# A two-layer transformer on one core: attention's outputs leave in three parts, the sums end later, the last heads go by block

## The chip, the core and the metric

One NeuronCore of a Trainium2 runs the whole program in one launch. Its engines each execute their own instructions in order and wait for each other by semaphores: TensorE (PE, matrix products), VectorE (DVE), ScalarE (ACT), GpSimd (POOL), and SyncE (SP), which here only issues transfers. Transfers (DMA) between memory (HBM) and on-chip SBUF run beside them. TensorE writes its products to PSUM, eight banks of 512 float32 a partition; GpSimd does not read PSUM in this program. The metric is the device time of one execution, the median of the runs.

## What is computed

Float32 throughout. An even layer over 2048 tokens (width 1024) with a context of 256 tokens that serves as extra keys, then an odd layer. In the even layer there are 8 heads with keys of their own (A) and 8 heads that share two sets of keys (B):

```python
sc = jnp.einsum('bqhgd,bthd->bhgqt', qi, k).astype(jnp.float32) * scale
p = jax.nn.softmax(sc, axis=-1).astype(v.dtype)
return jnp.einsum('bhgqt,bthe->bqhge', p, v)
...
merged = jnp.concatenate([o_a * jax.nn.silu(g_a), o_b * jax.nn.silu(g_b)], axis=-1)
return merged @ w_out
...
x_new = layer_norm(DEEPNORM_ALPHA * x + gate * y, ln_g, ln_b)
```

The odd layer is `chunk_gmlp`: `u`, `v`, `g` from one projection, a layer norm on `v`, a 128x128 mix of tokens inside each chunk, `u * mixed * silu(g)`, an output projection, again residual and layer norm.

## The kernel before

**Three stages.** `phase1` makes all projections of the even layer (keys, values, queries, gates) and leaves them in HBM. `attention` runs 64 groups, each a head `h` and a block of 512 queries `g`: first 32 groups of the 8 A heads ("first kind"), then 32 of the 8 B heads ("second kind"). `phase3` runs over 4 blocks of 512 tokens: even output projection, odd layer, output.

**Precision.** A float32 product is made of several passes of a rounded type: an operand is split into a high part and the rest (`split`: ACT rounds and DVE subtracts, or POOL does both), and the products high x high, high x low and low x high are added in PSUM.

**A group in `attention`.** The 2304 keys are 18 tiles of 128. For a tile `t`, `score` does three products (A) or two (B) of 512 columns into a PSUM tile `s` (three buffers); ACT takes the exponential twice, into `ph` (rounded) and back into `s` (exact); `low` has DVE subtract them into `pl`. That frees the score's tile. `mul`, four tiles later, multiplies values with both: `oh<-ph` (128 rows: the high part of the values in one half, the rest in the other) and `ol<-pl` (65 rows: a column of ones stands behind the values, so that row 64 collects the sum of the probabilities). The high parts' sum comes either from one more product with a matrix of ones (`ol<-ph,last`) or from GpSimd, which adds the `ph` tiles up (`add`, `sa<-sa,ph`) and splits the result at the end (`total`: sh by ACT, sl by POOL); PE then multiplies sh and sl with the ones at the end of `mul`'s last tile. Which tiles go which way stands in `shares`: its first list are tiles whose split GpSimd makes instead of DVE (`pf`, two operations), its second those that GpSimd adds; the last four groups have neither.

**The maxima.** A softmax needs its row's maximum ahead of the exponential. While group i-1 runs, PE makes plain products of group i's queries with its keys, 18 tiles `m` in two PSUM buffers (`peak`), and DVE takes maxima (`top`). After the last, DVE makes `nm`, which SP writes to HBM (`NM<-nm`, 512 separate elements) and reads back as a row of the query tile (`row`, `q<-NM`); the score products take it in as one more row (the only product of an A tile that needs it is the first, of a B tile the second).

**The end of a group.** `take` copies `ol` to `ob` (ACT), `finish` adds both halves of `oh` to it (two DVE operations), multiplies with the gate (POOL; the gate was loaded by SP) and SP writes the sums to `SU` and the output to `O`. When the last head is through a block of queries, `recip` loads that block's sums of all heads, inverts them (DVE) and writes `R1`. For block 0, `z_load` fetches output and inverse sums and `z_split` (POOL) multiplies and splits them, still inside `attention`.

**Order.** All of this is written as units with a time in tiles: `at(time, f, ...)`; the units are sorted by time and emitted. `InOrder` ties an engine's instructions into exactly that order, for PE, DVE, ACT and POOL. SP's transfers and all of `phase3` are ordered by the framework's own scheduler (by readiness and priority).

**`phase3`.** `weights` loads 512 KB of weights into `w` (two buffers) and splits it into `wh` (ACT) and `wl` (DVE), three buffers each; a tile serves 24 products. In `odd_in`, 16 such steps `j` follow; during them, the next block's outputs are fetched on GpSimd's queue (`z_load`), multiplied with the inverse sums and split (`z_split`, here on DVE), eight slices a block.

## Time and profile before

| | |
|---|---|
| three runs | 3239.22, 3242.19, 3242.39 us, median 3242.19 |
| the profiled execution | 3241.65 us, its span 3239.8 us, clock 0.994 |
| busy | PE 98%, DVE 77%, ACT 60%, POOL 46% of the span |

In forty slices of 81 us (a digit is the busy share in tenths) the stages can be told apart: `phase1` up to slice 8, attention to slice 28, with GpSimd busy, then `phase3`:

```profile
PE   7999999999999999999999999999999999999998
PEld 3887777777777777776666666666788888888886
DVE  4947794688898889888999999998655854855746
ACT  3544453377777777777777777777444353353352
POOL 2000100089999999998888888874100100100000
PEclk9999999999999999999999999999999999999999
DMA  6456746623212232122111111112633533533322
```

Line 636 in the profile stands for all of attention's ordered instructions (they go through one helper); tiles tell them apart. "PEld" is the loading of a matmul's fixed operand, which runs ahead of the product; a wait often stands there.

### The profile page before, as it was taken

What the parts mean: (1) busy time and instruction counts of PE and PEld (TensorE: products, weight loads), DVE (VectorE), ACT (ScalarE), POOL (GpSimd) and SP (SyncE); (2) the same over time, 40 slices, a digit from 0 to 9 for tenths busy, and PEclk for the clock granted to TensorE, in tenths of its full rate; (3) what the DMA queues carried; (4) which work ended last, traced back from release to release, by engine and by line L of the source; (5) the groups of instructions that cost most, each with busy time, mean ns of one, the idle gap of its engine ahead of it and who ended that gap; (6) DMA issues with size and microseconds to landing.
All of it is one profiled execution on the core that took longest, in us unless ns stands there. A gap on an engine that the chain in (4) does not pass through costs nothing.

```text
span 3239.8 us, 40308 instructions
## 1 busy us (share of the span) xinstructions
PE 3162.1 (98%) x13698; PEld 2422.8 (75%) x13698; DVE 2492.7 (77%) x3747; ACT 1935.2 (60%) x3306; POOL 1477.3 (46%) x1249
## 2 busy tenths in 40 slices
PE   7999999999999999999999999999999999999998
PEld 3887777777777777776666666666788888888886
DVE  4947794688898889888999999998655854855746
ACT  3544453377777777777777777777444353353352
POOL 2000100089999999998888888874100100100000
PEclk9999999999999999999999999999999999999999
DMA  6456746623212232122111111112633533533322
GB/s 239 141 170 192 249 158 212 177 69 66 62 38 49 62 65 46 41 62 62 30 29 25 30 47 30 30 25 61 172 98 111 151 110 111 163 101 114 117 91 72
DMA packets 187056, 314.08 MB, mean 97 GB/s; under 512 B 53264, under 2 KB 79184, under 8 KB 184928
## 3 DMA queue, kind: packets, MB, share of 16 engines
q1 hardware_dynamic: 178558, 283.62, 30.8%
q0 software_dynamic: 8000, 27.81, 2.9%
q8 instruction: 108, 1.77, 0.3%
q14 instruction: 100, 0.82, 0.1%
q10 hardware_dynamic: 290, 0.07, 0.0%
HBM read 240.71 MB, written 70.73 MB: 96 GB/s over the span
## 4 chain that ended last, share of the span: by engine, by line
PE 59%; DMA 13%; issue 12%; POOL 8%; DVE 7%; ACT 2%; SPq 0%; POOLq 0%; ACTq 0%; DVEq 0%
PE s L636 12%; DMA NM<-nm 7%; POOL sa L636 6%; PE ol L636 5%; PE ps L193 4%; PE ps L194 4%; PE ps L195 4%; PE oh L636 4%; PE m L636 4%; PE acc L967 3%; PE acc L968 3%; PE acc L969 3%; PE acc L1064 3%; PE acc L1062 3%; PE acc L1063 3%
## 5 line engine op out<-in xcount | busy, mean ns | idle before, releaser
L636 POOL TENSOR_TENSOR sa<-sa,ph 128x512 f32<-128x512 f32 x728 | 939.1, 1290 | 60.3 <-ACT ph L636 14.5
L636 PE MATMUL s<-q,k 96*128 96x512 f32 (+2 forms) x2880 | 873.9, 399 | 31.0 <-DVE pl L636 18.9
L636 ACT ACTIVATE ph<-s 128x512 fp32r<-128x512 f32 x1064 | 633.9, 596 | 303.7 <-PE s L636 284.4
L636 DVE TENSOR_TENSOR pl<-s,ph 128x512 fp32r<-128x512 f32 x1064 | 728.1, 685 | 109.0 <-ACT s L636 85.9
L636 DVE TENSOR_REDUCE mx<-m 128x1 f32<-128x512 f32 x1124 | 763.5, 681 | 57.8 <-PE m L636 54.1
L636 PEld LDWEIGHTS s<-q,k 96*128 96x128 f32 (+2 forms) x2880 | 537.3, 189 | 244.1 <-DVE pl L636 41.9
L636 ACT ACTIVATE s<-s 128x512 f32<-128x512 f32 x1064 | 632.8, 595 | 0.0
L636 PE MATMUL oh<-ph,v 128*128 128x512 f32 x1152 | 454.9, 395 | 0.0
L636 PE MATMUL ol<-pl,v 128*65 128x512 f32 x1152 | 454.8, 395 | 0.0
L636 PE MATMUL m<-k,q 128*128 128x512 f32 (+1 forms) x1250 | 449.1, 376 | 0.0
L67 ACT ACTIVATE wh<-w 128x1024 fp32r<-128x1024 f32 x153 | 162.1, 1060 | 455.0 <-PE acc L969 216.9
L68 DVE TENSOR_TENSOR wl<-w,wh 128x1024 fp32r<-128x1024 f32 x153 | 186.9, 1221 | 244.7 <-ACT wh L67 244.1
L636 PEld LDWEIGHTS m<-k,q 128*128 128x128 f32 (+1 forms) x1250 | 234.3, 189 | 67.5 <-DVE mx L636 14.5
L636 PEld LDWEIGHTS oh<-ph,v 128*128 128x128 f32 x1152 | 218.1, 189 | 48.9
L194 PE MATMUL ps<-xl,wh 128*128 128x512 f32 x608 | 238.4, 392 | 3.4 <-DVE xl L185 3.4
L193 PE MATMUL ps<-xh,wh 128*128 128x512 f32 x608 | 238.5, 393 | 2.9 <-POOL xh L184 2.9
L195 PE MATMUL ps<-xh,wl 128*128 128x512 f32 x608 | 237.8, 391 | 0.0
L636 PEld LDWEIGHTS ol<-pl,v 128*65 128x65 f32 x1152 | 157.5, 137 | 49.7 <-ACT ob L636 0.3
L967 PE MATMUL acc<-wh,k 128*128 128x512 f32 x384 | 152.6, 398 | 0.5 <-ACT v L1031 0.5
L968 PE MATMUL acc<-wl,k 128*128 128x512 f32 x384 | 152.4, 397 | 0.0
L969 PE MATMUL acc<-wh,k 128*128 128x512 f32 x384 | 151.6, 395 | 0.0
L194 PEld LDWEIGHTS ps<-xl,wh 128*128 128x128 f32 x608 | 114.6, 188 | 29.9 <-DVE xl L185 6.0
(319 smaller groups left out, 5054.6 us busy)
## 6 DMA issues: line engine op xcount, KB each, us to landing
w<-in_wug SPq DMA_DIRECT2D x64, 512.0 KB
wr<-in_w SPq DMA_DIRECT2D x38, 512.0 KB
w<-in_e_w_out SPq DMA_DIRECT2D x32, 512.0 KB
w<-in_o_w_in SPq DMA_DIRECT2D x32, 512.0 KB
w<-in_o_w_out SPq DMA_DIRECT2D x32, 512.0 KB
wr<-in_e_w_mod SPq DMA_DIRECT2D x24, 512.0 KB
wr<-in_o_w_mod SPq DMA_DIRECT2D x24, 512.0 KB
q<-QB SPq DMA_DIRECT2D x96, 128.0 KB
```

The source lines that it names most:

```text
L67: e.nc.scalar.activation(h, src, AF.Copy)
L68: e.nc.vector.tensor_tensor(out=l, in0=src, in1=h.bitcast(F32), op=ALU.subtract)
L193: nc.tensor.matmul(out, lhsT=wh(k), rhs=xh(k), start=i == 0, stop=False)
L194: nc.tensor.matmul(out, lhsT=wh(k), rhs=xl(k), start=False, stop=False)
L195: nc.tensor.matmul(out, lhsT=wl(k), rhs=xh(k), start=False, stop=i == n - 1)
L636: i = getattr(self.engine, name)(*args, **kw)
L967: nc.tensor.matmul(ps[t], lhsT=h[:, ts], rhs=w[0][:, k, :], start=first, stop=False)
L968: nc.tensor.matmul(ps[t], lhsT=h[:, ts], rhs=w[1][:, k, :], start=False, stop=False)
L969: nc.tensor.matmul(ps[t], lhsT=l[:, ts], rhs=w[0][:, k, :], start=False, stop=last)
L1062: nc.tensor.matmul(ps, lhsT=w[0][:, k, :], rhs=h, start=k == 0, stop=False)
L1063: nc.tensor.matmul(ps, lhsT=w[0][:, k, :], rhs=l, start=False, stop=False)
L1064: nc.tensor.matmul(ps, lhsT=w[1][:, k, :], rhs=h, start=False, stop=k == NK - 1)
```

## The change

1. *Sums.* `shares` has one list: GpSimd adds tiles 0 to 16 of a first-kind group and 0 to 15 of a second-kind one, and splits no tile (`pf` is gone; every tile has two exponentials and DVE's `pl`). `total` comes three tiles later. Its two products with the ones no longer go into `ol`: 9.1 tiles behind the last addition `sums` makes them in a PSUM tile of the maxima's ring (`m`, two buffers), ACT copies the row out (`os`) and SP writes it to a second array, `SU[1]`.
2. *Outputs.* `take` copies `ol` and SP writes it, with the sums of `ol`, to `O[0]` and `SU[0]`. One tile later `take_high` copies `oh` (ACT) and its halves go to `O[1]` and `O[2]`. DVE's two additions, GpSimd's product and the gate load are gone. `z_more` loads `O[1]`, `O[2]` and the gate of a slice (3 x 256 KB), and `z_split` has four operations ahead of the split where it had one: add, add, gate, inverse sum. In `phase3` the loaded tile `zx` has one buffer and its loads go on GpSimd's queue.
3. *Order.* The last four heads run block by block, their keys loaded once. Their `recip` is in two: the loads, and five tiles later addition, inversion and write (0.1 tiles later for the last block). Block 0's `z_load` and `z_split` start about a group earlier. SP's transfers in attention are held in the order of the units too.
4. *Last stage.* `wl` has two buffers instead of three; the residual's scale and shift move from the steps `j` to the evacuation of `v`; the steps at which slices are split are spread out (`zj`).

Beside this a constant of ones is set directly, and `ph` and `pl` have 9 buffers instead of 11.

```diff
-    q = queue or e.nc.sync
+    q = queue or e.sp
     t = t.bitcast(F32)
-    q.dma_start(t[:, :, 1, :], e.O[i * P:(i + n) * P, cs].rearrange("(k p) t -> p k t", p=P))
+    q.dma_start(t[:, :, 1, :], e.O[0][i * P:(i + n) * P, cs].rearrange("(k p) t -> p k t", p=P))
     for u in range(2):
         r = e.R1[2 * i:2 * (i + n), cs].rearrange("(k u) t -> u k t", u=2)[u]
         q.dma_start(t[u * DV:(u + 1) * DV, :, 0, :], r.partition_broadcast(DV))
 
 
-def z_split(e, hl, z, pool=False):
-    nc = e.nc
+def z_more(e, b, k, sp, queue=None, bufs=1):
+
+    t = sp.tile([P, 3, CH], F32, name="zx", tag="zx", bufs=bufs)
+    for i, src in enumerate(e.O[1:] + [e.G]):
+        (queue or e.sp).dma_start(t[:, i, :], src[k * P:(k + 1) * P, b * CH:(b + 1) * CH])
+    return t
+
+
+def z_split(e, hl, more, z, pool=False):
+
     h, l = hl
-    (pool or nc.vector).tensor_tensor(out=z, in0=l.bitcast(F32), in1=h.bitcast(F32), op=ALU.mult)
+    on = pool or e.nc.vector
+    on.tensor_tensor(out=z, in0=l.bitcast(F32), in1=more[:, 0, :], op=ALU.add)
+    on.tensor_tensor(out=z, in0=z, in1=more[:, 1, :], op=ALU.add)
+    on.tensor_tensor(out=z, in0=z, in1=more[:, 2, :], op=ALU.mult)
+    on.tensor_tensor(out=z, in0=z, in1=h.bitcast(F32), op=ALU.mult)
     split(e, h, l, z, pool)
...
-    PE, DVE, ACT, POOL = (InOrder(tc, x) for x in (nc.tensor, nc.vector, nc.scalar, nc.gpsimd))
-    LAG, LAGP = 4, 8
+    PE, DVE, ACT, POOL, SP = (InOrder(tc, x) for x in (nc.tensor, nc.vector, nc.scalar, nc.gpsimd, nc.sync))
+    e.sp = SP
+    LAG = 4
...
-        work = [(h, g) for h in range(2 * NH) for g in range(NG)]
+
+        work = [(h, g) for h in range(2 * NH - 4) for g in range(NG)]
+        work += [(h, g) for g in range(NG) for h in range(2 * NH - 4, 2 * NH)]
...
             if i >= NW - NG:
-                return (), ()
-            if i < NH * NG:
-                return (4,), tuple(t for t in range(17) if t != 4)
-            return (2, 8), tuple(t for t in range(16) if t not in (2, 5, 8, 12))
+                return ()
+            return tuple(range(17)) if i < NH * NG else tuple(range(16))
 
         def fetch_keys(h):
-            kv[h] = keys(e, h) if h < NH or h % 4 == 0 else kv[h - 1]
+            kv[h] = keys(e, h)
+            if h >= NH:
+                kv.update({k: kv[h] for k in range(h, h + 4)})
...
-            ph = sp.tile([P, CH], F32R, name="ph", tag="ph", bufs=LAGP + 3)
-            pl = sp.tile([P, CH], F32R, name="pl", tag="pl", bufs=LAGP + 3)
-            if t in shares(i)[0]:
-                ps, pf = sp.tile([P, CH], F32, name="pf", tag="pf", bufs=2), ps
-                ACT.activation(ps, pf, AF.Exp)
-            else:
-                ACT.activation(ph, ps, AF.Exp)
-                ACT.activation(ps, ps, AF.Exp)
+            ph = sp.tile([P, CH], F32R, name="ph", tag="ph", bufs=LAG + 5)
+            pl = sp.tile([P, CH], F32R, name="pl", tag="pl", bufs=LAG + 5)
+            ACT.activation(ph, ps, AF.Exp)
+            ACT.activation(ps, ps, AF.Exp)
             pts[s] = (ph, pl, ps)
 
         def low(s):
-            i, t = divmod(s, NTT)
             ph, pl, p = pts[s]
-            if t in shares(i)[0]:
-                POOL.tensor_scalar(out=ph, in0=p, scalar1=1.0, scalar2=0.0, op0=ALU.mult, op1=ALU.add)
-                POOL.tensor_tensor(out=pl, in0=p, in1=ph.bitcast(F32), op=ALU.subtract)
-            else:
-                DVE.tensor_tensor(out=pl, in0=p, in1=ph.bitcast(F32), op=ALU.subtract)
+            DVE.tensor_tensor(out=pl, in0=p, in1=ph.bitcast(F32), op=ALU.subtract)
 
         def add(s):
             i, t = divmod(s, NTT)
-            adds = shares(i)[1]
+            adds = shares(i)
...
-            if t not in shares(i)[1]:
+            if t not in shares(i):
                 PE.matmul(ol[:DV + 1], lhsT=last[:, :DV + 1], rhs=ph, start=False, stop=False)
             if end:
-                for p in tot.pop(i, ()):
-                    PE.matmul(ol[:DV + 1], lhsT=last[:, :DV + 1], rhs=p, start=False, stop=False)
                 PE.matmul(ol[:DV + 1], lhsT=V[:, t, DV:2 * DV + 1], rhs=pl, start=False, stop=True)
 
+        def cell(i):
+            h, g = work[i]
+            return h, slice(g * CH, (g + 1) * CH)
+
         def take(i):
-            ob = outs[i] = sp.tile([P, CH], F32, name="ob", tag="ob", bufs=2)
-            ACT.activation(ob[:DV + 1], acc[i][1][:DV + 1], AF.Copy)
-
-        def finish(i):
-            h, g = work[i]
-            cs = slice(g * CH, (g + 1) * CH)
-            ob, (oh, ol) = outs.pop(i), acc.pop(i)
-            DVE.tensor_tensor(out=ob[:DV], in0=oh[:DV], in1=ob[:DV], op=ALU.add)
-            DVE.tensor_tensor(out=ob[:DV], in0=oh[DV:], in1=ob[:DV], op=ALU.add)
-            POOL.tensor_tensor(out=ob[:DV], in0=ob[:DV], in1=gates.pop(i)[:DV], op=ALU.mult)
-            q = nc.scalar if i == NW - 1 else nc.sync
-            q.dma_start(e.SU[h:h + 1, cs], ob[DV:DV + 1])
-            (nc.gpsimd if i >= NW - NG else q).dma_start(e.O[h * DV:(h + 1) * DV, cs], ob[:DV])
+
+            (h, cs), (oh, ol) = cell(i), acc.pop(i)
+            rows = slice(h * DV, (h + 1) * DV)
+            q = nc.scalar if i == NW - 1 else SP
+            ob = sp.tile([P, CH], F32, name="ob", tag="ob", bufs=2)
+            ACT.activation(ob[:DV + 1], ol[:DV + 1], AF.Copy)
+            q.dma_start(e.SU[0][h:h + 1, cs], ob[DV:DV + 1])
+            q.dma_start(e.O[0][rows, cs], ob[:DV])
+            outs[i] = oh
+
+        def take_high(i):
+            (h, cs), oh = cell(i), outs.pop(i)
+            rows = slice(h * DV, (h + 1) * DV)
+            oc = sp.tile([P, CH], F32, name="oc", tag="oc", bufs=2)
+            ACT.activation(oc, oh, AF.Copy)
+            q = nc.gpsimd if i >= NW - NG else SP
+            for u in range(2):
+                q.dma_start(e.O[1 + u][rows, cs], oc[u * DV:(u + 1) * DV])
+
+        def sums(i):
+
+            pm = pp.tile([P, CH], F32, name="m", tag="m", bufs=2)
+            for u, p in enumerate(tot.pop(i)):
+                PE.matmul(pm[:DV + 1], lhsT=last[:, :DV + 1], rhs=p, start=u == 0, stop=u == 1)
+            tot[i] = pm
+
+        def sums_out(i):
+            h, cs = cell(i)
+            os = sp.tile([P, CH], F32, name="os", tag="os", bufs=2)
+            ACT.activation(os[DV:DV + 1], tot.pop(i)[DV:DV + 1], AF.Copy)
+            SP.dma_start(e.SU[1][h:h + 1, cs], os[DV:DV + 1])
 
         def recip(b):
 
             view = lambda t: t[:, b * CH:(b + 1) * CH].rearrange("h (p j) -> h p j", p=8)
-            rs = sp.tile([P, CH // 8], F32, name="rs", tag="rs", bufs=2)
-            q = nc.scalar if b == NG - 1 else nc.sync
-            q.dma_start(rs, view(e.SU))
-            nc.vector.reciprocal(rs, rs)
+            rs, r2 = rsums[b] = [sp.tile([P, CH // 8], F32, name="rs", tag="rs", bufs=4) for i in range(2)]
+            q = nc.scalar if b == NG - 1 else SP
+            q.dma_start(rs, view(e.SU[0]))
+            n = P if b < NG - 1 else P - 32
+            q.dma_start(r2[:n], view(e.SU[1])[:n // 8])
+
+        def recip_end(b):
+            view = lambda t: t[:, b * CH:(b + 1) * CH].rearrange("h (p j) -> h p j", p=8)
+            rs, r2 = rsums.pop(b)
+            q = nc.scalar if b == NG - 1 else SP
+            n = P if b < NG - 1 else P - 32
+            DVE.tensor_tensor(out=rs[:n], in0=rs[:n], in1=r2[:n], op=ALU.add)
+            DVE.reciprocal(rs, rs)
             q.dma_start(view(e.R1), rs)
...
+            adds = shares(i)
             at(s, score, s)
-            at(s + (0.9 if t in parts else 1.6), low, s)
+            at(s + 1.6, low, s)
             if t in adds:
                 at(s + 1.0, add, s)
             if adds and t == adds[-1]:
-                at(s + 1.1, total, i)
-            place = s + (LAGP if t in parts else LAG + (LATE[t] if t < len(LATE) else 0))
+                at(s + 4.1, total, i)
+                at(s + 9.1, sums, i)
+                at(s + 9.6, sums_out, i)
+            place = s + LAG + (LATE[t] if t < len(LATE) else 0)
             at(place + 0.7, mul, s)
             if t == NTT - 1:
                 at(place + 0.9, take, i)
-                at(place + 2.3, finish, i)
+                at(place + 1.9, take_high, i)
         for b in range(NG):
-            at((NW - NG + b + 1) * NTT + LAG + 2.6, recip, b)
+            time = (NW - 4 * (NG - 1 - b)) * NTT + LAG + (2.6 if b == NG - 1 else 6.1)
+            at(time, recip, b)
+            at(time + (0.1 if b == NG - 1 else 5), recip_end, b)
 
         end = NW * NTT
 
@@ -872,20 +908,28 @@
             e.Z.append(ring(e, more))
 
         e.Z = []
-        at(end - (NG - 1) * NTT - 1, place, False)
+        at(end - NG * NTT - 3, place, False)
         for k in range(3):
-            at(end - (NG - 1) * NTT + 9 + 4 * k, lambda k: z_load(e, 0, e.Z[0].groups[k]), k)
+            at(end - NG * NTT - 2 + 2 * k, lambda k: z_load(e, 0, e.Z[0].groups[k]), k)
 
         at(end - (NG - 2) * NTT + 0.8, lambda: extend(e.Z[0], spare(e)))
         at(end - (NG - 2) * NTT + 1, lambda: z_load(e, 0, e.Z[0].groups[3]))
+        more = {}
+
+        def other(k):
+            more[k] = z_more(e, 0, k, sp, bufs=2)
+
         for k in range(NK):
-            at(end - (NG - 1) * NTT + 4 * k + 17, lambda k: z_split(e, e.Z[0][k], sp.tile([P, CH], F32, name="zt", tag="zt", bufs=2), POOL), k)
+            time = end - NG * NTT + 7 * k + 8
+            at(time - 3, other, k)
+            at(time, lambda k: z_split(e, e.Z[0][k], more.pop(k), sp.tile([P, CH], F32, name="zt", tag="zt", bufs=1), POOL), k)
 
         e.marks = []
         for k in range(3):
             at(end - NTT + 5 * k, lambda: e.marks.append(POOL.last))
         for _, _, (f, *args) in sorted(units):
             f(*args)
+        e.sp = nc.sync
...
-            return wp.tile([P, 1024], F32R if q else F32, name="w" + q, tag="w" + q, bufs=3 if q else 2)
+            return wp.tile([P, 1024], F32R if q else F32, name="w" + q, tag="w" + q, bufs=3 if q == "h" else 2)
...
+                if cc == 0:
+                    nc.vector.tensor_tensor(out=T[:, t, :], in0=T[:, t, :], in1=C["eg"], op=ALU.mult)
+                    nc.vector.tensor_tensor(out=T[:, t, :], in0=T[:, t, :], in1=C["eb"], op=ALU.add)
...
+            zj = (2, 3, 5, 6, 8, 10, 12, 14)
...
-                    if 2 <= j < 10:
-                        z_split(e, Z[j - 2], tmp("y", 3))
+                    if j in zj:
+                        k = zj.index(j)
+                        z_split(e, Z[k], more, tmp("y", 3))
+                        if k + 1 < NK:
+                            more = z_more(e, b + 1, k + 1, wp, nc.gpsimd)
                     if j < len(Z.groups):
                         z_load(e, b + 1, Z.groups[j], nc.gpsimd)
-                if 4 <= j < 12:
-                    t = (j - 4) // 2
-                    nc.vector.tensor_tensor(out=T[:, t, :], in0=T[:, t, :], in1=C["eb" if j % 2 else "eg"], op=ALU.add if j % 2 else ALU.mult)
...
-    e.O = tc.dram_tile([D, SEQ], F32, name="O")
-    e.SU = tc.dram_tile([2 * NH, SEQ], F32, name="SU")
+    e.O = [tc.dram_tile([D, SEQ], F32, name="O%d" % i) for i in range(3)]
+    e.SU = [tc.dram_tile([2 * NH, SEQ], F32, name="SU%d" % i) for i in range(2)]
```

## Rows read from the trace of the kernel before

**Rows 1.** Busy time by stretch: us, busy us (x instructions) of PE, PEld, DVE, ACT, POOL; clock; DMA
```profile
1029.51:1081.68 52.17, 52.17 (x229) 40.23 (x228) 46.90 (x76) 39.87 (x74) 48.66 (x40) 1.00 0.22 47
1578.76:1675.87 97.11, 94.60 (x401) 67.41 (x401) 90.23 (x149) 76.72 (x144) 81.58 (x69) 1.00 0.12 28
2260.00:2280.00 20.00, 17.39 (x68) 11.96 (x68) 9.51 (x15) 13.06 (x25) 9.69 (x8) 0.91 0.22 63
2580.00:2600.00 20.00, 20.00 (x87) 15.98 (x87) 19.61 (x28) 9.14 (x14) 3.49 (x7) 1.00 0.75 235
2281.00:3239.80 958.80, 941.45 (x4192) 765.10 (x4191) 593.31 (x805) 394.57 (x532) 40.57 (x68) 0.99 0.40 119
```
**Rows 2.** Waits, 1554 to 2163 us: total us, times, longest us
```profile
PEld s L636 <- DVE pl L636: 24.4, 25, 1.0
...
PEld s L636 <- DMA q<-NM: 10.4, 16, 0.9
```
**Rows 3.** Timeline of PE: start, us, operation, [idle before and its releaser]
```profile
1810.59 0.50 PE L636 MATMUL s<-q,k 65*128 65x512 f32 x1 [0.23 <-DMA q<-NM]
...
1814.20 0.63 PE L636 MATMUL s<-q,k 128*128 128x512 f32 x2
...
1819.73 0.50 PE L636 MATMUL s<-q,k 128*128 128x512 f32 x1 [0.51 <-DVE pl L636]
```
**Rows 4.** Timeline of DVE, same group
```profile
1817.56 1.40 DVE L636 TENSOR_TENSOR ob<-oh,ob 64x512 f32<-64x512 f32 x2
1818.98 0.69 DVE L636 TENSOR_TENSOR pl<-s,ph 128x512 fp32r<-128x512 f32 x1
...
1822.70 0.17 DVE L636 TENSOR_REDUCE nm<-mx 128x4 fp32r<-128x20 f32 x1
```
**Rows 5.** The chain that ended last, 1797 to 1812 us: start, us, what
```profile
1798.29 0.19 DVE nm L636
...
1798.49 8.54 DMA NM<-nm
...
1807.04 3.51 DMA q<-NM
```
**Rows 6.** GpSimd's additions in the page's groups: busy us, mean ns
```profile
L636 POOL TENSOR_TENSOR sa<-sa,ph 128x512 f32<-128x512 f32 x728 | 939.1, 1290 | 60.3 <-ACT ph L636 14.5
```
**Rows 7.** Timeline of ACT, the group of rows 3
```profile
1816.74 0.59 ACT L636 ACTIVATE ph<-s 128x512 fp32r<-128x512 f32 x1
1817.22 0.59 ACT L636 ACTIVATE s<-s 128x512 f32<-128x512 f32 x1
```
**Rows 8.** Timeline of SyncE's queue in a first-kind head, issue times
```profile
977.36 0.42 SPq L672 DMA_DIRECT2D NM<-nm  x1
977.89 0.56 SPq L574 DMA_DIRECT2D v<-VA  x1
986.62 0.22 SPq L574 DMA_DIRECT2D q<-NM  x1
```
**Rows 9.** Timeline of DVE in the last group
```profile
2267.12 0.55 DVE L832 RECIPROCAL rs<-rs 128x64 f32<-128x64 f32 x1 [4.02 <-DMA rs<-SU]
```
**Rows 10.** Timeline of PE in the last group
```profile
2252.48 0.51 PE L636 MATMUL s<-q,k 65*128 65x512 f32 x1 [1.54 <-DMA q<-NM]
...
2268.27 0.93 PE L636 MATMUL s<-q,k 128*128 128x512 f32 x2 [2.19 <-DVE pl L636]
```
**Rows 11.** Timeline of SyncE's queue, a weight load at a block boundary
```profile
2566.15 0.37 SPq L941 DMA_DIRECT2D w<-in_o_w_in  x1
```
**Rows 12.** Timeline of DVE in a quiet stretch of the last stage
```profile
2413.84 1.23 DVE L68 TENSOR_TENSOR wl<-w,wh 128x1024 fp32r<-128x1024 f32 x1 [4.21 <-ACT wh L67]
```
**Rows 13.** Timeline of ACT, the conversion that uses the load of rows 11
```profile
2579.94 1.06 ACT L67 ACTIVATE wh<-w 128x1024 fp32r<-128x1024 f32 x1 [1.98 <-DMA w<-in_o_w_in]
```
**Rows 14.** DMA issues: KB each, median us from issue to landing
```profile
v<-in_x POOLq DMA_DIRECT2D x8, 512.0 KB, 6.2
...
k<-O POOLq DMA_DIRECT2D x3, 1024.0 KB, 11.0
```

More of the change, by code (lines that the diff above doesn't have):

```diff
@@ L48, in consts @@
     nc.sync.dma_start(e.ident, I["ident"])
-    e.ones = g.tile([P, P], F32, name="ones")
-    nc.vector.memset(e.ones, 1.0)
     e.epsq = {S: g.tile([P, 1], F32, name="eps%d" % i) for i, S in enumerate((1.0, SA, SB))}
@@ L100, in phase1 @@
         ones = cp.tile([P, P], F32R, name="ones")
-        nc.scalar.activation(ones, e.ones, AF.Copy)
+        nc.vector.memset(ones.bitcast(F32), 1.0)
         pick = cp.tile([P, 2, 2], F32, name="pick")
@@ L563, in z_load @@
         q.dma_start(t[u * DV:(u + 1) * DV, :, 0, :], r.partition_broadcast(DV))
-def z_split(e, hl, z, pool=False):
-    nc = e.nc
-    h, l = hl
-    (pool or nc.vector).tensor_tensor(out=z, in0=l.bitcast(F32), in1=h.bitcast(F32), op=ALU.mult)
+def z_more(e, b, k, sp, queue=None, bufs=1):
[4 more added lines that the diff above has]
+def z_split(e, hl, more, z, pool=False):
+    h, l = hl
+    on = pool or e.nc.vector
[3 more added lines that the diff above has]
+    on.tensor_tensor(out=z, in0=z, in1=h.bitcast(F32), op=ALU.mult)
     split(e, h, l, z, pool)
 def load(e, dst, src):
-    e.nc.sync.dma_start(dst.bitcast(F32), src)
+    e.sp.dma_start(dst.bitcast(F32), src)
 def keys(e, h, parts=3, KV=None):
@@ L671, in peak_maxima @@
         DVE.tensor_reduce(out=nm, in_=stats.pop(i), axis=AX.X, op=ALU.max, negate=True)
-        e.nc.sync.dma_start(e.NM[i:i + 1, :].rearrange("o (j p) -> p (o j)", p=P), nm.bitcast(F32))
+        e.sp.dma_start(e.NM[i:i + 1, :].rearrange("o (j p) -> p (o j)", p=P), nm.bitcast(F32))
 def peak_row(e, h, i, Q):
@@ L705, in attention @@
         NG = SEQ // CH
-        work = [(h, g) for h in range(2 * NH) for g in range(NG)]
+        work = [(h, g) for h in range(2 * NH - 4) for g in range(NG)]
+        work += [(h, g) for g in range(NG) for h in range(2 * NH - 4, 2 * NH)]
         NW = len(work)
-        kv, qs, stats, pms, pts = {}, {}, {}, {}, {}
+        kv, qs, stats, pms, pts, rsums = {}, {}, {}, {}, {}, {}
         acc, tot, gates, outs = {}, {}, {}, {}
@@ L794, in mul @@
             if t == 0:
-                gates[i] = sp.tile([P, CH], F32, name="gt", tag="gt", bufs=2)
-                nc.sync.dma_start(gates[i][:DV], e.G[h * DV:(h + 1) * DV, g * CH:(g + 1) * CH])
                 acc[i] = [pp.tile([P, CH], F32, name="o" + q, tag="o" + q, bufs=1 + (q == "h")) for q in "hl"]
@@ L844, in attention @@
                 at((i - 2) * NTT + 1.2, fetch_queries, i)
-            if i % NG == 1 and i // NG + 1 < 2 * NH:
-                at(i * NTT + 1.2, fetch_keys, i // NG + 1)
+            h = i // NG + 1
+            if i % NG == 1 and (h <= NH or h == NH + 4):
+                at(i * NTT + 1.2, fetch_keys, h)
             for m in range((NTT, AHEAD)[i] if i < 2 else 0, NTT):
@@ L853, in attention @@
             i, t = divmod(s, NTT)
-            parts, adds = shares(i)
+            adds = shares(i)
             at(s, score, s)
-            at(s + (0.9 if t in parts else 1.6), low, s)
+            at(s + 1.6, low, s)
             if t in adds:
@@ L1077, in odd_in @@
                 if b + 1 < NB:
-                    if 2 <= j < 10:
-                        z_split(e, Z[j - 2], tmp("y", 3))
+                    if j in zj:
[3 more added lines that the diff above has]
+                            more = z_more(e, b + 1, k + 1, wp, nc.gpsimd)
                     if j < len(Z.groups):
                         z_load(e, b + 1, Z.groups[j], nc.gpsimd)
-                if 4 <= j < 12:
-                    t = (j - 4) // 2
-                    nc.vector.tensor_tensor(out=T[:, t, :], in0=T[:, t, :], in1=C["eb" if j % 2 else "eg"], op=ALU.add if j % 2 else ALU.mult)
+                    if j == 0:
+                        more = z_more(e, b + 1, 0, wp, nc.gpsimd)
             gated(7, st)
@@ L1152, in program @@
     e.nc, e.ins, e.out = nc, ins, out
+    e.sp = nc.sync
     with tile.TileContext(nc) as tc:
```

## The prediction

> **What bounds the kernel now.** The page comes first, but its busy shares settle little: a matmul's record runs past the issue of the next, so a busy PE can hide a wait. I therefore counted issues by stretch. Two groups of a first-kind head take 52.17 us for 228 matmuls (the row's count has one of the next group), 8 of them half wide, so 224 full ones at 0.233 us; PE is busy throughout, it alone sets the time. Four groups of a second-kind head take 97.11 us for 400 matmuls, 392 full ones, which at 0.233 us need 91.3 us: each group takes 24.28 us and loses 1.45 us. The last stage, 959 us, has PE busy 941 us: PE is the bound there [rows 1].
>
> Next the waits of PE in 25 second-kind groups: score products wait for VectorE's (DVE's) `pl`, since a score's PSUM tile is free only after it, and for the row of maxima, `q<-NM` [rows 2]. The timeline of one group places them: 0.51 us idle before the product at 1819.73, and a second product at 1810.59 behind the row [rows 3]. The first is DVE's: it does the two `ob` additions (1.40 us) and only then `pl` at 1818.98 [rows 4]. The second is a chain of transfers: `nm` at 1798.29, its transfer 8.54 us, reading it back 3.51 us; the product goes 12.30 us behind `nm` [rows 3, 5]. The next `nm` comes 12.11 us after that product [rows 3, 4], and 12.11 + 12.30 is the group's 24.41 us. So a second-kind group is a ring: product, `nm`, two transfers, next product. A saving counts in full between the product and `nm`; between `nm` and the next product it only lengthens the wait.
>
> **First-kind heads.** GpSimd (POOL) adds 17 tiles' probabilities instead of 16, so one ones-product goes: 112 full matmuls become 111, 0.233 us in each of 32 groups, **-7.5 us**. PE stays the bound if the others fit into 25.9 us. GpSimd will have 16 additions and the tail's difference, an operation of the same form, 17 x 1.29 = 21.9 us [rows 6]. ScalarE (ACT) issues every 0.48 to 0.49 us [rows 7]; 40 operations (36 exponentials, sh, ob, oc, os) are 19.6 us. Without that cover each us over 25.9 counts 32 times. The saved product lies behind `nm`, but the ring has slack here: the row's transfer took 9.26 us even with the loading of a head's keys and values around it [rows 8], and at PE's own pace there are 25.9 us to go round.
>
> **Second-kind heads.** Four ones-products go (tiles 2, 5, 8 and 12 are now added too): 94 full matmuls, 21.9 us. GpSimd fits with 16 x 1.29 = 20.6 us. DVE swaps two `ob` additions for two `pl`, 37 operations either way. But the four products lie between `nm` and the next product, where the ring has no use for them: nothing by themselves. What counts is `nm`, and I follow it from the score of tile 3 (1814.20; call it 0, then `nm` was at 8.50 [rows 3, 4]). The tail's two products are later now, so score 4 goes at 1.40 instead of 1.84. ScalarE does ob, the two exponentials of tile 4, oc, and those of tiles 5 and 6 at 0.49 us apart; tile 4's second ends at 3.28. DVE, without `ob`, does pl 4 at 3.3, the maximum at 3.9, pl 5 at 4.9 (ScalarE is late by its oc), a maximum, pl 6 at 6.1, the last maximum at 6.85 and `nm` at 7.55. On the way the sums take one of the two maxima tiles: the next product needs the other, which DVE has read at 4.65 and PE wants at 4.19, 0.45 us of PE wait that DVE's own chain mostly covers. So `nm` comes 0.95 us earlier. Bounds: at best the whole 1.40 us of the `ob` additions; at worst the two extra copies before that point (0.98) and the 0.45 us take it all, and it comes 0.03 us later. I take 0.93, the chain's value with a little off. The transfers I leave at 12.3 us: SyncE had an O part and the gate load ahead of NM, it will have three O parts and a second row of sums. 27 steady groups: **-25.1 us** (from +1 to -38). A group is then 23.35 us where PE needs 21.9 + 0.5, so its wait at the row grows to some 0.95 us: the row is what is late next.
>
> The Trainium skill ("DMA: Bandwidth & Descriptors", Anatomy of one DMA) puts a transfer's fixed cost near 2.0 us. By it the two would cost some 4 us and the row would never bind; here the 8.54 us for 512 separate elements decides, four times that.
>
> **The last four groups.** `recip` blocked DVE for its load, 4.02 us idle before `rs` [rows 9]; PE waited 2.19 us for `pl` [rows 10], and the granted clock of those 20 us was 0.91, 1.8 us more [rows 1]. The load now goes out five tiles ahead, so 4.0 us go. Against it SyncE, now held in written order, issues the first block's parts (three loads for each slice) ahead of two of the maxima rows: beside heavy loads the row took 9.26 against 8.54 us [rows 5, 8], +0.7, and three issues at 0.37 us [rows 11] are +1.1. Net **-2.2 us** (from -4, nothing lost, to +4, where both rows stand behind the 3.3 us that 768 KB take at 235 GB/s [rows 1] and their issues). GpSimd's longer gate-and-add of eight slices (each five operations of 1.29 us and a conversion) lies in 72 tiles in which it adds nothing else.
>
> **The last stage.** Three more DVE operations for each of 24 slices, 24 x 3 x 0.6 = 43 us, on an engine busy 593 of 959 us [rows 1]: hidden, unless they stand in front of a weight split. That cover gets thinner: `wl` has two buffers, not three. In a quiet stretch `wl` goes as soon as ScalarE's half is there, 4.21 us idle and 1.23 us of work, one in 5.44 us [rows 12]. With a buffer fewer it must end within about those 4.2 us, and a raw weight load has one tile less to arrive: 3 x 5.44 less the two conversions (1.06 + 1.23) and the split before its issue (1.23), 12.8 us. At the boundary of a block a load took 13.8 us from issue to use [rows 11, 13], with the transfer engines 75% busy [rows 1]: 1.0 us of PE wait at each of two boundaries. The new parts add 768 KB there, 3.3 us at that stretch's 235 GB/s. So from 2.0 to 8.6 us; I take **+6**, nearer to the upper end because the new loads start in that same burst. The moved T operations, the constant of ones and the vanished gate loads I cost at nothing: they lie on engines that idle at those places, and if these did not idle they would be a few us.
>
> **Sum.** -7.5 - 25.1 - 2.2 + 6 = -28.8 us. From the profiled execution's 3241.65 us (span 3239.8 and 1.85 around it) 3212.9; the median of the runs is 0.54 above that execution: **3213 us**.
>
> **Rivals.**
> 1. ScalarE gives it back: oc, os and the maxima tile leave `nm` only 0.2 us earlier. For: scores already wait for DVE at this place. Against: ScalarE has 19.6 us of work in 23. 27 x 0.73 = 19.7: **3233**.
> 2. The row stops binding (its transfer is quicker once an O part and the gate load are not right ahead of it): groups fall to PE's 22.4 us, 24.28 - 22.4 = 1.9, x 27 = 51 instead of 25: **3187**. Against: 8.54 us with only small transfers about.
> 3. Slower: DVE stands in order at the first addition of a slice until that slice's parts have landed, since `zx` has one buffer and its next load starts only when DVE has read the last. Loads from GpSimd's queue took 6.2 us for 512 KB and 11.0 us for 1 MB [rows 14]; over the 4.2 us of cover that is 2.0 to 6.8 us, for the four slices of each of three blocks that can run back to back: 12 x 4.4 = 53 us on top of 3213 less my 6: **3260**. It decides once the excess passes 35/12 = 2.9 us, a landing of 7.1 us. Against: the later slices are spread over two weight tiles each.
> 4. Clock: a fall behind the longer wait in each second-kind group, at 1.8 us as above, 27 x 1.8 = 49: **3262**. PE waited 1.54 us at 2252.48 and 2.19 us at 2268.27 [rows 10]; only the second stretch shows a granted clock under 1, and my wait is 0.95. [...]
> 5. The change does nothing in second-kind groups: the new transfers ahead of the row make it later by what `nm` gains. 3213 + 25 = **3238**.
>
> **Chances.** Forecast 0.58 (own range 3200 to 3226), rival 1 0.14, 2 0.11, 3 0.10, 4 0.03, 5 0.04. Range 3188 to 3240: it leaves out rivals 3 and 4 and about half of 2. A measurement of this kernel can tell about 0.2%, 6.5 us: faster 0.58 + 0.11 + 0.09 of rival 1 = 0.78; same 0.05 + 0.04 = 0.09; slower 0.13.
>
> **What would show it.** First-kind groups 25.85 us apart; second-kind ones 23.35, no PE wait for `pl` behind a group's end, `nm` 11.2 us behind the product, the product still 12.3 us behind `nm` with a wait near 1 us; no DVE idle before `rs` in the last groups but the very last; PE waits for `wl` of a few us at two block boundaries. Wrong if the time from `nm` to the product changes, if PE waits for ScalarE's os, or if DVE idles at `zx`.

## The result, and the profile after

The changed kernel takes 3265.39 us (median of 4 runs, 3262.73 to 3269.09), the kernel before, beside it, 3241.39: a ratio of 1.0076, 95% interval 1.0058 to 1.0093. It is slower by 24 us; 3213 was forecast.

From the page of the changed kernel: the span, the engines' busy time and the shares of the chain that ended last.
```profile
span 3261.0 us, 41089 instructions
...
PE 3140.3 (96%) x13554; PEld 2417.9 (74%) x13554; DVE 2532.1 (78%) x3783; ACT 2027.2 (62%) x3508; POOL 1490.2 (46%) x1253
...
PE 59%; DMA 16%; issue 11%; DVE 7%; ACT 5%; POOL 2%; SPq 1%; ACTq 0%; POOLq 0%; DVEq 0%
```
PE lost share of a longer span; 16% of the chain are transfers. Which transfers, only the stretches tell. I cut every run at the starts of ScalarE's copy `ob` of groups 0, 31, 59 and 63. Each stretch in us, of the profiled execution:

| kernel | first stage | first-kind heads | second-kind | last four groups | last stage | ratio of runs to before [95%] |
|---|---|---|---|---|---|---|
| before | 681.6 | 813.6 | 686.5 | 99.3 | 958.7 | |
| changed | 682.0 | 824.3 | 667.9 | 103.8 | 983.0 | 1.0076 [1.0058, 1.0093] |
| 1 free order | 680.7 | 806.3 | 662.9 | 120.0 | 993.6 | 1.0067 [1.0055, 1.0079] |
| 2 queries first | 680.7 | 811.2 | 670.1 | 103.1 | 992.5 | 1.0046 [1.0034, 1.0058] |
| 3 before, `wl` 2 | 678.0 | 814.4 | 688.1 | 99.1 | 973.7 | 1.0024 [1.0015, 1.0032] |
| 4 no parts, `wl` 3 | 679.3 | 817.7 | 672.3 | 103.8 | 966.9 | 1.0001 [0.9992, 1.0009] |
| 5 GpSimd adds | 678.2 | 826.8 | 668.2 | 103.4 | 993.7 | 1.0096 [1.0080, 1.0112] |
| 6 free, moved loads | 681.2 | 804.8 | 664.6 | 143.1 | 991.3 | 1.0145 [1.0130, 1.0161] |
| 7 both | 681.3 | 804.1 | 663.9 | 143.9 | 988.0 | 1.0154 [1.0138, 1.0170] |
| 8 and AHEAD 11 | 681.7 | 801.0 | 637.1 | 139.6 | 991.3 | 1.0050 [1.0038, 1.0063] |
| 9 pieces, `wl` 3 | 680.6 | 817.1 | 671.0 | 99.6 | 967.4 | 1.0025 [1.0014, 1.0036] |
| 10 all | 679.9 | 801.0 | 635.7 | 92.9 | 971.9 | 0.9828 [0.9815, 0.9841] |
| 11 all but the last stage | 682.3 | 801.0 | 636.0 | 93.0 | 990.5 | 0.9893 [0.9880, 0.9906] |
| 12 before, AHEAD 11 | 680.8 | 813.0 | 672.0 | 99.7 | 958.0 | 0.9962 [0.9950, 0.9974] |

The same last stage took 983 to 994 us in the changed kernel, 1, 2, 6 and 11, and the same attention took 817 to 827 us for its first-kind heads in the changed kernel, 4, 5 and 9. So one profile tells such a stretch to some 10 us; where that decides, I go by the ratios.

The change's span is 21.2 us longer: first-kind heads +10.7, second-kind heads -18.6, last four groups +4.5, last stage +24.3. The forecast had -7.5, -25.1, -2.2 and +6: each stretch is over it, by 18.2, 6.5, 6.7 and 18.3 us.

Two steady groups of a first-kind head (answering the first line of [rows 1]), then all first-kind heads, the second-kind stretch and the last stage. Columns as in [rows 1].
```profile
922.81:974.48 51.67, 51.67 (x227) 39.98 (x226) 46.56 (x74) 42.63 (x81) 45.80 (x36) 1.00 0.14 31
682.00:1506.00 824.00, 810.25 (x3500) 623.48 (x3499) 722.54 (x1147) 660.56 (x1241) 695.49 (x545) 0.99 0.26 58
1506.20:2174.20 668.00, 634.15 (x2688) 461.46 (x2688) 627.40 (x1041) 594.32 (x1122) 575.42 (x449) 0.99 0.18 41
2278.00:3261.00 983.00, 946.02 (x4192) 763.62 (x4190) 643.92 (x876) 385.11 (x525) 80.03 (x140) 0.99 0.46 136
```
A steady first-kind group takes 25.84 us, with PE busy throughout: what the step on the ones-product forecast (25.85). The steady second-kind group, PE's and then DVE's timeline:
```profile
1782.66 0.50 PE L646 MATMUL s<-q,k 65*128 65x512 f32 x1 [0.61 <-DMA q<-NM]
...
1805.99 0.50 PE L646 MATMUL s<-q,k 65*128 65x512 f32 x1 [0.46 <-DMA q<-NM]
```
```profile
1793.96 0.17 DVE L646 TENSOR_REDUCE nm<-mx 128x4 fp32r<-128x20 f32 x1
```
`nm` comes 11.30 us behind the product, the next product 12.03 us behind `nm`: 23.33 us, against 12.11 and 12.30 before [rows 3, 4]. Over 25 groups the medians are 11.29 and 12.21, against 12.10 and 12.32. So both attention terms hold in the steady groups. What was lost lies elsewhere.

**First loss: the order of SyncE's queue.** SyncE in the first-kind head whose successor's keys are fetched, then PE:
```profile
1201.48 0.62 SPq L646 DMA_DIRECT2D k<-KA  x1
1202.16 0.59 SPq L646 DMA_DIRECT2D k<-KR  x1
1202.85 0.57 SPq L646 DMA_DIRECT2D v<-VA  x1
1203.51 9.33 SPq L646 DMA_DIRECT2D q<-QN  x1
1212.90 0.59 SPq L646 DMA_DIRECT2D q<-QP  x1
```
```profile
1219.02 0.47 PE L646 MATMUL m<-k,q 96*128 96x512 f32 x1 [2.70 <-DMA q<-QP]
```
Keys and values (1152 + 576 + 1152 KB) are written ahead of the queries of the group after next. The issue of these queries alone takes 9.33 us, and PE, which wants them for the first maxima, waits 2.70 us. Behind the wait it ran at a lower granted clock:
```profile
1219.00:1223.30 4.30, 4.28 (x13) 3.24 (x14) 2.67 (x4) 1.09 (x2) 2.02 (x2) 0.66 0.07 3
```
0.66 is a mean of the two levels, 1.2 and 2.4 GHz. The eight groups in which keys are fetched took 26.6 to 30.4 us, some 23 us more than eight steady ones. PE's waits for queries are 12.5 us of it. PE was busy 810.3 us in these heads where 801.0 do for the same products (run 10, below), so some 9 us more, by this estimate, are the lower clock behind the waits.

**Second loss: group 60**, 37.8 us long. SyncE, PE and DVE:
```profile
2166.17 0.38 SPq L646 DMA_DIRECT2D k<-O  x1
...
2168.61 1.69 SPq L646 DMA_DIRECT2D v<-R  x2
2170.34 4.76 SPq L646 DMA_DIRECT2D q<-QB  x3
...
2189.20 3.23 SPq L646 DMA_DIRECT2D rs<-SU  x2
```
```profile
2184.47 0.77 PE L646 MATMUL m<-k,q 128*128 128x512 f32 x1 [3.61 <-DMA q<-QB]
...
2201.12 0.80 PE L646 MATMUL m<-k,q 128*128 128x512 f32 x1 [2.87 <-DVE mx L646]
```
```profile
2199.60 0.33 DVE L646 TENSOR_TENSOR rs<-rs 128x64 f32<-128x64 f32 x1 [3.51 <-DMA rs<-SU]
```
The queries (`QB`) stand behind the first loads of the projection's input (`O`, `R`), and DVE still stands at the reciprocal's load (before: 4.02 us, [rows 9]). It does so in group 56 too, which took 28.6 us:
```profile
2092.26 0.37 DVE L646 TENSOR_TENSOR rs<-rs 128x64 f32<-128x64 f32 x1 [3.83 <-DMA rs<-SU]
```

**Third loss: the last stage**, waits of PE for the low half of a weight, of ScalarE for the weight itself, and of DVE for the parts (total us, times, longest):
```profile
PE acc L1012 <- DVE wl L66: 10.4, 8, 2.0
PE acc L1112 <- DVE wl L66: 6.4, 4, 2.3
...
ACT wh L65 <- DMA w<-in_wug: 45.3, 17, 4.7
...
DVE y L577 <- DMA zx<-O: 10.4, 8, 2.1
```
In the kernel before, PE did not wait for `wl` at all. Nearly all these waits lie in three stretches, those in which the first parts of a block are loaded every 7.7 us beside the weights. One of them, and the quiet stretch behind it, in the columns of [rows 1]:
```profile
2580.00:2640.00 60.00, 53.51 (x225) 41.49 (x224) 48.71 (x70) 27.11 (x37) 10.80 (x20) 1.00 0.68 194
2640.00:2820.00 180.00, 179.64 (x809) 145.43 (x808) 117.32 (x159) 70.26 (x97) 13.51 (x24) 1.00 0.44 129
```
With the transfer engines 68% busy PE loses 6.5 of 60 us; at 44%, 0.4 of 180. The other two (2370 to 2385, 2825 to 2870) lose 3.0 and 6.9: 16.4 us in all.

### The profile page after: what moved, and what is told of

It is laid out like the page before. It is cut to its first block, busy times and chain, and to the rows that moved or that the text cites. A ratio compares the mean times of both kernels' runs of the same rounds, so it can differ in the third digit from the quotient of the medians.

```text
span 3261.0 us, 41089 instructions
## 1 busy us (share of the span) xinstructions
PE 3140.3 (96%) x13554; PEld 2417.9 (74%) x13554; DVE 2532.1 (78%) x3783; ACT 2027.2 (62%) x3508; POOL 1490.2 (46%) x1253
## 4 chain that ended last, share of the span: by engine, by line
PE 59%; DMA 16%; issue 11%; DVE 7%; ACT 5%; POOL 2%; SPq 1%; ACTq 0%; POOLq 0%; DVEq 0%
PE s L646 14%; PE ol L646 6%; PE m L646 6%; DMA NM<-nm 6%; PE oh L646 5%; PE ps L191 4%; PE ps L192 4%; PE ps L193 4%; PE acc L1112 2%; PE acc L1110 2%; PE acc L1111 2%; PE acc L1012 2%; PE acc L1011 2%; DMA q<-NM 2%; PE acc L1013 2%
## 5 line engine op out<-in xcount | busy, mean ns | idle before, releaser
L646 POOL TENSOR_TENSOR sa<-sa,ph 128x512 f32<-128x512 f32 x872 | 1123.6, 1288 | 86.0 <-ACT ph L646 21.3
L646 PE MATMUL s<-q,k 96*128 96x512 f32 (+2 forms) x2880 | 873.3, 399 | 17.4 <-DMA q<-NM 16.4
L646 DVE TENSOR_TENSOR pl<-s,ph 128x512 fp32r<-128x512 f32 x1152 | 792.4, 688 | 105.7 <-ACT s L646 62.1
L646 ACT ACTIVATE ph<-s 128x512 fp32r<-128x512 f32 x1152 | 688.4, 598 | 268.5 <-PE s L646 236.5
L646 PEld LDWEIGHTS s<-q,k 96*128 96x128 f32 (+2 forms) x2880 | 547.9, 191 | 212.4 <-DMA q<-NM 26.0
L646 ACT ACTIVATE s<-s 128x512 f32<-128x512 f32 x1152 | 686.3, 596 | 0.0
L646 PE MATMUL m<-k,q 128*128 128x512 f32 (+1 forms) x1250 | 456.3, 381 | 37.8 <-DVE mx L646 17.4
L568 POOL DMA_DIRECT2D zx<-O x48 | 25.7, 540 | 332.7 <-DVE y L578 332.7
```

What stands on the lines that cost most here:

```text
L646: i = getattr(self.engine, name)(*args, **kw)
```

## The experiments

Theory 1: the written order of SyncE's queue costs the attention's gain, and `wl` with two buffers and the added parts cost the last stage. Rival: it is the load on the transfer engines, whatever the order.

**1, free order.**
```
-    PE, DVE, ACT, POOL, SP = (InOrder(tc, x) for x in (..., nc.sync))
+    PE, DVE, ACT, POOL = (InOrder(tc, x) for x in (...))
+    SP = nc.sync
```


> The changed kernel, but SyncE's transfers are not held in the written order any more; the other engines are. Theory 1 (the written order of SyncE's queue puts a head's keys, the parts and the reciprocal's rows ahead of the queries that TensorE needs next): the eight first-kind groups in which the next head's keys are fetched fall from 26.6 to 30.4 us to about 26, which takes some 18 us out of the stretch of the first-kind heads (824 to about 806), group 60 falls from 37.8 us towards 27, and the time falls from 3265 to 3230 to 3240. Rival (the long groups come from the load on the DMA engines itself, or from the ring of the maxima): the order changes nothing, the groups stay over 26.5 us, and the time stays within 5 us of 3265. Both leave the last stage at about 983 us.

The heads did what theory 1 says (806.3 and 662.9 us; the eight groups 25.8 to 25.9). The time did not: 3263.5, because the last four groups took 120 (the last stage, untouched, came out 10 us longer in this profile). DVE and PE there:
```profile
2171.88 1.30 DVE L646 TENSOR_TENSOR rs<-rs 128x64 f32<-128x64 f32 x1 [6.35 <-DMA rs<-SU]
```
```profile
2174.37 0.80 PE L646 MATMUL m<-k,q 128*128 128x512 f32 x1 [6.68 <-DVE mx L646]
...
2197.03 0.77 PE L646 MATMUL m<-k,q 128*128 128x512 f32 x1 [6.09 <-DMA q<-QB]
```
The parts' loads, which wait for GpSimd to free their buffers, now stood on SyncE ahead of rows and queries. So "free order repairs the attention" holds for the heads alone.

**2, queries first.** `at(i * NTT + 1.2, fetch_keys, h)` becomes `1.3`.

> The changed kernel with one place changed: the next head's keys are asked for at tile 1.3 of the group instead of 1.2, so that the queries of the group after next stand ahead of them on SyncE's queue, which is otherwise held in the written order. Theory 1: this alone takes the stall at the start of the following group away, some 18 us in the first-kind heads (824 to about 806) and about 4 us in group 45, and the time falls from 3265 to about 3243; groups 56 and 60 keep their length. Rival (load on the DMA engines): the keys move the same 2.9 MB and what follows them is late all the same, the stall moves to the next row of maxima, and the time stays within 5 us of 3265.

3253.4, heads 811.2: one place in the written order gives back 12 us of the time, and 13 of the 18 us by these two profiles. What stays is the row of maxima, which now stands behind the keys (PE waits 5.5 us for it in all; groups 21 and 25 still took 28.0 and 30.2). Group 45 gained nothing to speak of (27.0). The first-kind stretch moves the same bytes in the changed kernel, 1 and 2 (58, 60 and 60 GB/s), so the order is the cause and not the load.

**3, before with two `wl` buffers**, `bufs=3 if q == "h" else 2`.

> The kernel before, with the low half of a weight in two buffers instead of three, as the change has it, and nothing else. If the third buffer is what the last stage lacks: the stage grows from 959 us by 15 to 25, and the time is 3255 to 3265. If the loss of the last stage comes from the added parts (VectorE's additions and their transfers): the time stays within 4 us of 3241.

3246.95, +0.24%: 7 us, between what the two sides had. A buffer fewer costs by itself, but not 24.

**4, no parts.** `2 <= j < 10` as before, no `z_more`, `wl` three buffers: blocks 1 to 3 leave out two of the three parts and the gate.

> The changed kernel, but the last stage of blocks 1 to 3 takes the projection's input as the kernel before did: the other two parts and the gate are neither loaded nor added there (left out of the computation for these blocks), and the room goes into the third buffer of the weight's low half. Both theories of the last stage: it goes back to about 959 us and the time to about 3241. If the last stage lost its 24 us to something before it (the clock, or the loads left over by the attention), it stays near 983 and the time near 3265. With the run on the kernel before with two buffers this tells buffers from parts.

3238.67: the last stage's loss is there, 27 us between this run and the changed kernel by the medians, 24 by the ratios. Its last stage is still 8 us over that of the kernel before, which one profile can't tell from nothing; whether the moved scale and shift cost any of it was not tested.

**5, GpSimd adds the parts.**
```
-                        z_split(e, Z[k], more, tmp("y", 3))
+                        z_split(e, Z[k], more, None, nc.gpsimd)   # in place, in zx
```


> The changed kernel, but in blocks 1 to 3 of the last stage GpSimd adds the two parts, gates, multiplies and splits, in place of VectorE and ScalarE; the weight's low half keeps its two buffers. Theory 1 (the parts cost because VectorE stands in order at a part that has not landed, or does 50 us more of work, while the low half of a weight is late): of the last stage's 24 us the part that the run without parts and the run with two buffers leave to the parts, 17 to 20, comes back, and the time falls from 3265 to about 3247. Rival (the parts' transfers cost, or GpSimd's longer instructions, 1.3 us against 0.69, make the projection's input late): the stage stays within 5 us of the changed kernel's, and the time at 3260 or above.

Theory 1's version here, that DVE standing at a part or its added work makes `wl` late, fell: DVE neither adds nor waits for parts, and PE's wait for `wl` grew.
```profile
PE acc L1014 <- DVE wl L66: 14.1, 8, 4.7
PE acc L1114 <- DVE wl L66: 7.5, 5, 2.8
...
ACT wh L65 <- DMA w<-in_wug: 93.5, 25, 7.5
```
By these rows the weight itself is late: ScalarE's wait for its load is twice that of the changed kernel.

**6, free order, moved loads; 7, with 5 as well.**
```
-            more[k] = z_more(e, 0, k, sp, bufs=2)
+            more[k] = z_more(e, 0, k, sp, POOL, bufs=2)
-            at(time + (0.1 if b == NG - 1 else 5), recip_end, b)
+            at(time + (0.1 if b == NG - 1 else 12), recip_end, b)
```


> The changed kernel with SyncE's transfers not held in order, and two more places changed: the loads of the other parts for the projection's first block are issued on GpSimd's queue, ahead of the additions that use them, and the reciprocal's addition stands 12 tiles behind its loads instead of 5. Theory 1 (groups 60 and 61 of the run with a free order, 35 and 42 us, are a SyncE queue that stands at the parts' buffers while the rows and queries wait behind): the last four groups fall from 120 to about 95 to 100, the heads stay at 806 and 663, and the time falls from 3263.5 to about 3240. Rival (the traffic of these loads is what makes rows and queries late, on whatever queue): the last four groups stay over 110 us and the time over 3255. The last stage is the changed kernel's in both.

> The two edits before together: free order on SyncE, the first block's parts on GpSimd's queue, the reciprocal later, and GpSimd adding the parts in blocks 1 to 3. If the losses are separate, as theory 1 has them, they add: about 3265 less 25 less 18, that is 3222, faster than both kernels. If they share a cause (traffic on the DMA engines), the sum falls short: 3235 or more.

Groups 60 and 61 came to 25.9 and 25.8 us, so that part of theory 1 stands, but group 62 took 72.6 (74.0 in 7): a new wait in the place of the old. Both times are over the changed kernel's (3285.83 and 3286.19), and 7 tells nothing on whether losses add.

**8, AHEAD 11 on top of 7.**

> As the run with both edits, with AHEAD 11 instead of 10: the products for the maxima of a group start one tile earlier, and with them the maxima's row. Theory (in the second-kind groups TensorE stands 0.5 to 0.9 us at the row and 0.48 at the ring of the maxima's tiles; the first goes, the second stays): the groups fall from 23.4 to about 22.9, 28 of them by 14 us in all, and the time to about 3208. Rival (the queries, of which the first product needs the last at tile 7.6 instead of 8.6, or the ring, come in the row's place): the groups stay at 23.4 or grow, and the time is within 4 us of the run with both edits or above.

3254.18. Against 7 the time fell by 32 us, over twice the forecast: groups of 22.6, not 22.9. PE's wait for the row is gone and the ring's small one stays. The stretch of the second-kind heads, and then group 62, on SyncE and PE:
```profile
1482.70:2119.80 637.10, 624.14 (x2688) 461.30 (x2687) 620.38 (x1040) 594.81 (x1122) 577.07 (x451) 1.00 0.22 46
```
```profile
2209.24 0.41 SPq L988 DMA_DIRECT2D w<-in_e_w_out  x1
...
2229.90 0.24 SPq L586 DMA_DIRECT2D q<-NM  x1
```
```profile
2232.91 0.79 PE L648 MATMUL s<-q,k 65*128 65x512 f32 x1 [45.19 <-DMA q<-NM]
```
The scheduler had put two weight loads of the last stage ahead of the last row of maxima; a load's buffer waits for GpSimd, which was late with the parts, and everything behind it on SyncE's queue stood.

**9, pieces and three `wl` buffers.** GpSimd loads each part by itself (2 KB a partition, two buffers) and adds it; `y` two buffers; `wl` three.
```
-                        z_split(e, Z[k], more, tmp("y", 3))
+                        more.split(k)    # add, add, load, gate, load, multiply, split, load
-  bufs=3 if q == "h" else 2
+  bufs=3 if q else 2
```


> The changed kernel with its attention untouched; in the last stage GpSimd adds the parts one piece at a time (two buffers of 2 KB in place of one of 6), VectorE's scratch tile y has two buffers instead of three, and the room gives the weight's low half its third buffer back. Theory 1 (the last stage's loss is the two buffers' cover, too short once the parts' transfers make weight loads later): the stage falls from 983 to 960 to 967 and the time from 3265 to about 3243. Rival (the parts' traffic alone delays the weights, whatever the cover): the stage stays over 978 and the time over 3258.

3246.48 (12 runs, 3237.0 to 3254.6), 19 us under the changed kernel by the medians and 16 by the ratios, with the same bytes added. The rival (traffic, whatever the cover) fell. But the pieces also spread the loads: in the stretches that answer to the three above (92, 302 and 547 us into the stage) the transfer engines were 43, 58 and 62% busy, against 67, 68 and 71%. How much is the third buffer's and how much the thinner burst's was not told apart.

**10, all together**: 8 with the last stage of 9, the first block's parts loaded one step earlier, and the first weight loads behind the last row:
```
-            at(time - 3, other, k)
+            at(time - 8 if k else time - 3, other, k)
+            if after: tc.add_manual_dep(d.ins, e.row, ...)   # weights(): behind the last q<-NM
```
**11**, the same with the changed kernel's last stage.

For run 10:

> The run with AHEAD 11, with the last stage as in the run of pieces, the first block's parts loaded one step earlier, and the first three weight loads of the last stage held behind the last row of maxima on SyncE's queue. If group 62's 70 us (a row of maxima that stood behind a weight load which waited for GpSimd) is that order and nothing else: the last four groups fall from 140 to about 96, the stage to about 965, heads and second-kind groups stay at 801 and 637: 682 + 801 + 637 + 96 + 965 = 3181, and 3183 with what lies around the span. If the last stage stays at 985: 3203. If the order of the weight loads has nothing to do with it: over 3225.

For run 11:

> As the run before, but with the changed kernel's last stage (VectorE adds the parts, two buffers of the low half). It tells what the last stage costs beside an attention without the order's losses: 682 + 801 + 637 + 96 + 983 = 3199, and 3201 with what lies around the span, if the parts cost the 24 us found before; about 3180 if the loss was brought by the attention's end and not by the last stage itself.

3182.71 (run 10) and 3203.41 (run 11), both within 3 us of the forecast. Run 10 is 1.7% faster than before. Its stretches, in the order of the table from the first-kind heads on:
```profile
679.90:1480.90 801.00, 801.00 (x3501) 619.04 (x3500) 723.77 (x1147) 660.82 (x1241) 696.39 (x545) 1.00 0.32 59
1480.90:2116.60 635.70, 623.75 (x2688) 461.59 (x2687) 620.14 (x1040) 594.70 (x1121) 576.58 (x451) 1.00 0.21 46
2116.60:2209.60 93.00, 92.10 (x400) 66.21 (x399) 72.37 (x114) 77.29 (x147) 82.45 (x83) 1.00 0.48 125
2209.60:3181.50 971.90, 943.58 (x4192) 764.58 (x4190) 614.47 (x756) 382.77 (x509) 291.76 (x282) 0.99 0.45 136
```
PE is busy without a gap in the first-kind heads. The last four groups are 47 us shorter than in 8, about the 45.19 us that PE stood at the row there. Two edits could have done it, the weight loads behind the row and the parts a step earlier; no run parts them. Between 11 and 10 only the last stage differs, 20.7 us; of PE's waits for `wl` there (15.3 us in 11), this is left in 10:
```profile
PE acc L1045 <- DVE wl L66: 0.3, 1, 0.3
```

**12, before with AHEAD 11.**

> The kernel before with AHEAD 11 instead of 10 and nothing else. If its second-kind groups (24.5 us) are bound by the wait for the row of maxima alone, which the earlier products shorten by a tile: they fall to about 23.5, the stretch by 28 and the time to about 3213. If VectorE's queue is what holds them there (outputs and halves of exponentials stand before the maxima, as the working has it), nothing or little comes: within 5 us of 3240.

3225.79, between the two: groups fell to 24.0, not 23.5. The row's wait is gone, and the weight loads of PE wait for DVE as long as before [rows 2]:
```profile
PEld s L636 <- DVE pl L636: 24.4, 25, 1.0
```
PE's own wait for `pl` stays too (12.3 us over 25 groups, 12.4 before), while its 5.3 us at the row are gone. This fits the working, by which the two `ob` additions and the row each bind the kernel before; a tile more lead gets only the row's share. The change's own edits take the rest, 24.0 to 22.6, of which the four ones-products are 0.9; no run takes the `ob` additions away alone.

## Why the prediction was wrong

**Right.** The ones-product: 26.09 to 25.84 us in each of 32 groups, 8.0 us, against 7.5. The ring of a second-kind group: medians of 24.43 and 23.51 us, 0.92 each, against 0.93. That it fits so closely is in part luck: `nm` came 0.81 us earlier, and the transfers, left as they were in the forecast, took 0.11 less. PE's row wait is 0.55 us on average where 0.95 was forecast, and 0.31 goes to the maxima's ring. ScalarE (rival 1) and nothing gained (rival 5) didn't happen.

**Wrong: SyncE "held in written order".** The step priced this at +0.7 and +1.1, for the last four groups alone. It holds in all 64 groups: keys stand ahead of queries where the queue was free to mix them, and that was never followed, though the working itself looked at a queue with a head's keys in it [rows 8]. It took 18 us from the first-kind heads (run 1 against the changed kernel; 11 to 21 against the four profiles of that attention), some 5 from the second-kind ones, and in group 60 it put queries behind the projection's input. Rows 8 show the free order, in which a row was issued right behind the values; they don't bear on the written one.

**Wrong: the reciprocal's -4.0.** The step took a lead of five tiles, about 6.5 us, to cover the load. In group 56 it was issued at 2080.77 and DVE went on at 2092.26, 11.5 us later, having stood 3.83 us. In group 60 it was issued only at 2189.20, behind the parts, and DVE stood 3.51 us. At the very end DVE stood 8.8 us, against 5.6 before.

**Wrong: the last stage's +6** (2.0 to 8.6). The step had named the cause, 12.8 us for a weight load with one buffer fewer, but let it bind once, for 1.0 us, at each of two block boundaries, and let the parts add their bytes once. It bound 12 times, 16.8 us in all, all but one in three stretches of 15 to 60 us, where a new slice's parts come every 7.7 us. By medians: 7 us for two buffers without parts (3 against before); 8 for parts with three (9 against 4); 27 for both (the changed kernel against 4; 24 by the ratios). So the two together seem to cost more than their sum, though 3 is a run of the kernel before, and 9 also spreads the loads and moves the adding to GpSimd; that move alone, with two buffers (5), gained nothing. VectorE adding with three buffers was not tried.

**Rival 3** had its mechanism in part: DVE did stand at `zx`, one of the prediction's own signs of being wrong, 24.4 us over 21 waits, none over 2.5 us. But run 5, without these waits, was no faster.

**Rival 4's clock** did not fall at the row's 0.5 us. It fell beside nine single waits of 1.79 to 4.27 us in the changed kernel's attention (0.66 at 1219, 0.72 after 2201), and not at four of 1.10 to 1.53 us; in run 2 it fell at one of 1.56 us and not at one of 1.91. So it came in through the long waits, which the forecast did not have. The Trainium skill ("TensorE: Matmul & The Clock Gate", HAM oscillation) describes PE falling cold at long DMA waits that recur in a loop. The trace agrees at five of the eight key-fetching groups. The row's waits recur too, but are several times shorter than those of the skill's case, and left the clock at 1.00 (1717 to 1788 us, three second-kind groups).

## What to carry to other kernels

Before holding a DMA queue in a written order, list for each transfer what is queued ahead of it and who waits for what is behind: large loads with slack go behind small ones without it, and a load whose buffer another engine frees does not belong on a queue that carries a loop's critical row. Giving up a buffer and adding traffic are to be priced together: each alone cost 7 to 8 us here, both 24 to 27. And once a ring of waits has been found, try its lead first: one more tile of it was worth 12 us on the kernel before and 32 on run 7, most of it in the second-kind heads.

## What the runs showed of the hardware

An issue is not always cheap: behind 2.9 MB of loads SyncE took 9.33 us to issue one of 256 KB, against 0.37 us for a weight load by itself [rows 11]. In seven first-kind groups of the changed kernel this issue took 8.1 to 9.5 us, in the other 21 it took 0.6. In run 2, where the same queries go first, it took 0.6 everywhere, and the 2 KB of sums that then came next behind the keys took 4.9 to 5.9. So here the time goes with the place in the queue and not with the load that is issued. The Trainium skill ("DMA: Bandwidth & Descriptors", Issuing engines are not separate DMA queues) calls the time that issuing takes usually small beside the transfer; the row differs, and PE's wait of 2.70 us for the queries lies behind it.
